# Score products over 128 contraction rows: padded low parts of the keys and padded rotary tiles

## The chip, the core and the metric

The kernel runs on one core of a Trainium2 chip. Its engines are TensorE (matrix products; PE in the profile, its weight loads PEld), VectorE (DVE), ScalarE (ACT), GpSimd (POOL) and SyncE (SP), which issues most of the transfers. The metric is the device time of one execution in microseconds; the median of the runs counts.

## The reference

A sequence of 512 tokens with 1024 channels passes through two small transformer blocks of two layers each. Each layer is a mixer and a gated feed-forward net with a convolution of width three. The mixers are a state-space layer (S5), the Fox attention, a chunk attention and a latent attention (MLA). All three attentions have 16 heads of 64 channels. Their scores, in short:

```python
# Fox: causal, with a decay per head and position
s = einsum('bhqd,bshd->bhqs', q, k) + F[q] - F[k];  p = softmax(where(causal, s, -inf))
# chunk attention: a bias by distance, keys of the own and the earlier chunks
s = einsum('bhqd,bkhd->bhqk', q, k) * 64**-0.5 + bias;  p = softmax(where(valid, s, NEG_INF))
# MLA: 64 channels of each head and 32 rotary channels, whose key is one for all heads
s = (einsum('bqhd,bkhd->bhqk', qn, kn) + einsum('bqhd,bkd->bhqk', qr, kr)) * 96**-0.5
```

In each the probabilities then multiply the values, and the result is projected back to 1024 channels.

## The kernel before

Activations lie with channels on the 128 partitions and the 512 tokens along the columns. Every product is taken with operands split into a rounded high part and a low part that holds the rest. The large projections add three products (high by high, high by low, low by high; `mm3`, lines 373 to 375).

For the scores, a head has only 64 channels, and the three terms are packed. `proj_q` makes one tile per head: the high part of q on the head's own half of the partitions (64 rows) and the low part on the other half. `proj_k` makes a tile `y` per head with the high part of k on both halves, so that one product over 128 rows (line 561) gives high by high and low by high. The remaining term, high q by low k, is a product over 64 rows (line 565) that reads the head's half of q's tile and of `z`, a tile that holds the low parts of both heads of a pair. In MLA a product over 96 rows (line 564) stands between them: rotary query `r` (32 rows high, 32 low, 32 high again) by rotary key `kr` (64 rows high, 32 low). `Head.scores` does this for four query blocks; block `qb` sees 128 * (qb + 1) keys, so the products have 128, 256, 384 and 512 columns. All terms of a block add up in one bank of the accumulation memory. VectorE then adds bias and mask and takes the maximum (lines 570, 573, 576), ScalarE takes the exponential (586), VectorE normalises (592), and `values` transposes the probabilities (605, ScalarE copies them at 608) and multiplies them with the values (615, products with 64 output columns).

`Mixer` sets the order: 16 heads in 8 pairs, a pair's values after the first scores of the next pair, and after each head 1.5 (Fox, chunk) or 1.75 (MLA) units of projection for later pairs. A unit is one `proj_q`, one `proj_k`, half a `proj_v`, or in MLA a `uqr`, which makes the rotary queries of four heads. The order within each engine is fixed when the program is built; an engine works through its own queue in that order and waits at an instruction until its operands and its buffer are there.

The tiles of q, k, v and the rotary queries come from the pool `gp` with 28 buffers of 128 x 512; in Fox and chunk attention the results of the heads lie there too, in MLA the latent inputs. ScalarE writes the high part (line 520), GpSimd copies it to the other half (521), VectorE subtracts for the low part (522). In `uqr` the same three are lines 1526, 1527 and 1528.

Of the kernel before, what the change touches and what calls it, by code (L numbers as in the profile page):

```python
# [9 lines left out]
F32 = mybir.dt.float32  # L10
F32R = mybir.dt.float32r
# [75 lines left out]
def tile_two_blocks(ctx, tc, ap, out):  # L87
# [15 lines left out]
    # ---------------------------------------------------------------- constants  # L103
# [20 lines left out]
    # ---------------------------------------------------------------- adaLN columns  # L124
# [15 lines left out]
    def ada(name, first, cb, m, bias, key, n=24):  # L140
        """Queue one layer's columns: shift and scale, then the gate."""
        items = ada_items(name, first, n, cb, m)
        for part, a, b in (("", 0, min(16, n)), ("gate", 16, n)):
            if a < b:
                def done(a=a, b=b, part=part):
                    dve.tensor_add(m[:, a:b], m[:, a:b], bias[:, a:b])
                    finished.add(key + part)
                background.extend(items[a:b] + [done])
# [12 lines left out]
    # ---------------------------------------------------------------- rms norm  # L161
    class Norm:
        """Running sum of squares over channel tiles, then 1/rms spread over all partitions."""
# [55 lines left out]
    class TwoNorms(Norm):  # L219
        """A norm with gains g, and 1/rms of its result times that of the norm itself."""  # L220
# [56 lines left out]
    def modulate(h, rb, A, B, alloc=None):  # L277
        """(h * rstd) * A + B per channel tile, as hi and lo parts."""
        X = []
        for k in range(len(h)):  # L280
            a, b = A[:, k:k + 1], B[:, k:k + 1]
            t = tmp.tile([P, S], F32, name="t0")
            hi, lo = (alloc or pair)()
            dve.scalar_tensor_tensor(t, h[k], a, rb, op0=OP.mult, op1=OP.mult)  # L284
            act.activation(hi, t, AF.Identity, bias=b)
            if k % 2:
                dve.scalar_tensor_tensor(lo, t, b, hi.bitcast(F32), op0=OP.add, op1=OP.subtract)
            else:
                v = tmp.tile([P, S], F32, name="t1")
                act.activation(v, t, AF.Identity, bias=b)  # L290
                pool.tensor_tensor(lo, v, hi.bitcast(F32), OP.subtract)  # L291
            X.append((hi, lo))
        return X
# [4 lines left out]
    class Ahead:  # L298
        """Products with A h taken while 1/rms is on its way: W^T (r A h + B) = r W^T (A h) + W^T B."""
# [15 lines left out]
        def products(self, jobs, norm=None):  # L315
            """jobs: (pool, name, weights) each."""
# [30 lines left out]
    # ---------------------------------------------------------------- weights  # L347
# [29 lines left out]
    def gemm(ps, src, kts, X, cols=P, eng=dve, seq=None, shift=None, then={}, loaded=None):  # L377
        """ps[cols, S] (+)= W^T X for the channel tiles kts; src is the DRAM tile [P, len * cols]."""
# [31 lines left out]
    # ---------------------------------------------------------------- load x, c  # L410
    h = [hp.tile([P, S], F32, name=f"h{k}") for k in range(KD)]

    def affine(m, shift, scale, g, name):
        """A = g * (1 + scale)"""
        A = late[0].tile([P, KD], F32, name="A_" + name)
        dve.scalar_tensor_tensor(A, m[:, scale:scale + KD], 1.0, g, op0=OP.add, op1=OP.mult)
        return A, m[:, shift:shift + KD]

    def project_out(src, X, gate, norm=None, ready=None, early=0, perm=False):
        """h += gate * (W^T X); ready() gives what the next products need, asked for before channel tile early."""  # L420
# [22 lines left out]
    # ---------------------------------------------------------------- feed-forward  # L443
    def ffn(gp, ahead, norm, wup, wdn, cw, cb, both, gate, last, aside=None):
        """cw(tap, channel tile) and cb(channel tile) give columns; both: the second half is convolved too."""
# [41 lines left out]
    # ---------------------------------------------------------------- attention  # L487
# [7 lines left out]
    def start_attention(ahead, norm, *srcs):  # L495
        """The first projections before 1/rms, then the modulated input."""
        ps = ahead.products([(pl, name, w) for w, (pl, name) in zip(srcs, ((ps_mm, "mm"), (ps_s, "s")))],
                            norm)
        X = modulate(h, ahead.rb, ahead.A, ahead.B)
        return X, [lambda i=i, p=p: ahead.value(p, i) for i, p in enumerate(ps)]  # L500

    def proj_q(ps, scale):
        """Per head of a pair: hi rows at the head's own half of the partitions, lo rows at the other."""
# [9 lines left out]
    def proj_k(ps):  # L513
        """Per head hi rows on both halves; lo rows of both heads in one tile."""
        z = gp.tile([P, S], F32R, name="g")
        out = []
        for hh in range(2):
            a, b = HALF[hh], HALF[1 - hh]
            y = gp.tile([P, S], F32R, name="g")
            act.activation(y[a], ps[a], AF.Copy)  # L520
            pool.tensor_copy(y[b], y[a].bitcast(F32))
            dve.tensor_sub(z[a], ps[a], y[a].bitcast(F32))
            out.append(y)
        return out, z

    def proj_v(src, kts, X, half, wts):
        """Token-major values of two pairs of heads, for the two token tiles of a half."""
# [18 lines left out]
    class Head:  # L546
        """One head: scores and softmax, then transposed probabilities times values."""

        def scores(self, hh, x, y, z, bias, bias_d, scale, extra=None, fq=None):
            a = HALF[hh]  # L550
# [6 lines left out]
            for qb in range(4):  # L557
# [7 lines left out]
                pe.matmul(s, x[a, qs], z[a, :n], start=False, stop=True)  # L565
# [28 lines left out]
    def values(heads, v, cols, dst):  # L594
        """Transposed probabilities times values for a pair of heads, each on its half of the partitions."""
# [24 lines left out]
    class Mixer:  # L620
        """Pairs of heads: a pair's values after the next pair's first scores, projections of later pairs in between."""
# [32 lines left out]
    # ---------------------------------------------------------------- polynomial helpers  # L654
    def stt(eng, work, out, a, c, b, op0, op1):
        """(a op0 c) op1 b"""
# [7 lines left out]
    def sincos(eng, pl, x, shape, tag, work=None, s=None, v=None):  # L664
        """(sin x, 1 - cos x) with x fp32."""
# [39 lines left out]
    # ================================================================ block 1, layer 0: S5  # L705
# [5 lines left out]
    class Later:  # L711
        """Stands for an engine: keeps its instructions for a chosen place among others."""
# [7 lines left out]
    def merge(*lists):  # L720
        """Issue lists of instructions side by side, each spread evenly."""
# [4 lines left out]
    with tc.block(schedule_with_timeline_sim=TIMELINE):  # L726
# [35 lines left out]
        # the input, and shift and scale of its modulation: a quarter of the row on each quarter of the partitions  # L762
# [20 lines left out]
        # parameters: Lambda^a, the factor of B, the rotations of the chunks  # L783
# [48 lines left out]
        # 1/rms  # L832
# [6 lines left out]
        # e^{i 8 theta n}, n < 64: groups 8 q .. and 32 + 8 q .. on the two halves of the partitions  # L839
# [85 lines left out]
        def rotations(q, dve):  # L925
# [4 lines left out]
            for i in range(6):  # L930
                m = 1 << i
                for a in range(2):
                    # real part: c re - s im; imaginary part: c im + s re
# [11 lines left out]
        class Tables:  # L945
            """Tables of groups 8 i .. 8 i + 7."""
# [35 lines left out]
            def for_c(self, eng):  # L982
                """C L^a, a = 0 .. 8"""
# [3 lines left out]
            def for_b(self, eng):  # L987
                """B L^(7 - j)"""
# [17 lines left out]
            def on_pe(self):  # L1006
# [6 lines left out]
                # kernels of the lags 0 .. 7, then shifted copies of them  # L1013
# [20 lines left out]
        def inputs(tab, U):  # L1034
            """What every chunk adds to the states, and the same with real and imaginary parts swapped."""
# [8 lines left out]
        def states(tab, sab):  # L1044
            """The states at the chunks' ends in the turning frame."""
# [15 lines left out]
        def back(tab, wz):  # L1061
            """... and rotated back."""
# [139 lines left out]
    def more_weights(n):  # L1202
        """Room for more tiles of weights while no heads are at work."""
# [45 lines left out]
    # ================================================================ block 1, layer 0: FFN  # L1249
# [12 lines left out]
    # ================================================================ block 1, layer 1: Fox  # L1262
# [20 lines left out]
    # log sigmoid(x) = min(x, 0) - 2 atanh(e / (2 + e)), e = exp(-|x|)  # L1283
# [37 lines left out]
    def qkv_units(wq, wk, wv, X, scale, first):  # L1321
        """Projection units in the order in which the heads need them: src(i) per pair, src(j) per two pairs for v."""
# [18 lines left out]
    def fox_head(t, cur):  # L1341
# [7 lines left out]
        cur.scores(hh, Q[i][hh], K[i][0][hh], K[i][1], b, bd, 1.0, fq=Fq[:, :, t])  # L1349
# [14 lines left out]
    # ================================================================ block 1, layer 1: FFN  # L1364
# [15 lines left out]
    # ================================================================ block 2, layer 0: chunk attention  # L1380
# [17 lines left out]
    def chunk_head(t, cur):  # L1398
# [5 lines left out]
        cur.scores(hh, Q[i][hh], K[i][0][hh], K[i][1], bias_t.pop(t), None, 1.0)  # L1404
# [20 lines left out]
    # ================================================================ block 2, layer 0: FFN  # L1425
# [23 lines left out]
    # ================================================================ block 2, layer 1: MLA  # L1449
# [3 lines left out]
    def rope(t, dst):  # L1453
        """Rotated by the angles of the positions."""
# [33 lines left out]
    kr = rp.tile([96, S], F32R, name="kr")  # L1488
# [29 lines left out]
    def uqr(j):  # L1518
# [4 lines left out]
        for a in range(4):  # L1523
            r = gp.tile([P, S], F32R, name="g")
            src = ps[32 * a:32 * a + 32]
# [35 lines left out]
    def mla_head(t, cur):  # L1561
        i, hh = t // 2, t % 2
        cur.scores(hh, Q[i][hh], K[i][0][hh], K[i][1], mask0, None, SC, extra=(QR.pop(t)[0:96], kr))
        return V[i // 2]
# [11 lines left out]
    # ================================================================ block 2, layer 1: FFN, final norm  # L1576
    g = col("final_g_2", 0, KD)

    def to_end(src, X, gate):
        """The last two channel tiles by halves of the tokens, so that a half's norm runs beside products."""  # L1580
# [128 lines left out]
```

## Time and profile before

| | |
|---|---|
| median of 3 runs | 2748.35 us (2745.33 to 2751.65) |
| span of the profiled execution, first to last instruction | 2740.6 us |
| busy: TensorE matmuls | 2601.1 us, 95% |
| busy: VectorE, ScalarE, GpSimd | 1791.4 us (65%), 1144.3 us (42%), 359.8 us (13%) |
| mean granted clock of TensorE | 0.968 of full |

The profile shows one execution. Its own time was not recorded beside its span; the span is some 8 us under the median of the runs, and that difference is what lies around the first and the last instruction. Matmuls overlap and their ends are modelled, so the busy time of TensorE says how long something was under way, not how fast it went; the distance between two starts tells the latter.

### The profile page before, as it was taken

To read this page: it belongs to the slowest core of one execution; us is meant where nothing else is said; L and a number is where in the kernel's file an instruction comes from. 1 tells how busy PE (TensorE), PEld (TensorE's weight loads), DVE (VectorE), ACT (ScalarE), POOL (GpSimd) and SP (SyncE) were. 2 spreads that over 40 slices of the span, in tenths; PEclk is the share of its full clock that TensorE was granted. 3 is DMA by queue.
4 is the path that set the end of the run, shared out by engine and by line. 5 is a ranking of instruction groups with operands and counts; after the bars stand their busy time and mean duration, and the time that the engine had idled before them with its cause. 6 is when DMAs were issued, how large, how long until landed. Compare 5 with 4: busy or idle time off the path is not lost.

```text
span 2740.6 us, 32676 instructions
## 1 busy us (share of the span) xinstructions
PE 2601.1 (95%) x11970; PEld 2026.6 (74%) x11970; DVE 1791.4 (65%) x3199; ACT 1144.3 (42%) x1904; POOL 359.8 (13%) x331
## 2 busy tenths in 40 slices
PE   3787989999999999999999999999999899999998
PEld 1576768888867767888887777788888566788887
DVE  9897885455576658646566556985766665763554
ACT  2443353233354554323344554532334566542342
POOL 7562100000021100000011010650000110000000
PEclk7878989999999999999999999999999999999999
DMA  5445654443332334455433323445542111323322
GB/s 202 116 119 133 230 183 131 146 142 123 99 108 96 97 107 160 154 168 183 140 105 103 112 92 116 148 150 175 169 140 91 31 35 54 100 86 94 106 78 76
DMA packets 131120, 335.66 MB, mean 122 GB/s; under 512 B 37008, under 2 KB 41872, under 8 KB 130960
## 3 DMA queue, kind: packets, MB, share of 16 engines
q1 hardware_dynamic: 129232, 331.74, 38.4%
q8 instruction: 94, 1.54, 0.2%
q10 hardware_dynamic: 1728, 1.84, 0.2%
q14 instruction: 66, 0.54, 0.1%
HBM read 320.68 MB, written 6.29 MB: 119 GB/s over the span
## 4 chain that ended last, share of the span: by engine, by line
PE 80%; DVE 9%; issue 4%; DMA 2%; POOL 2%; ACT 2%; SPq 0%; POOLq 0%; ACTq 0%; DVEq 0%
PE mm L373 17%; PE mm L374 17%; PE mm L375 17%; PE s L373 6%; PE s L374 6%; PE s L375 6%; PE aux L615 3%; PE pt L605 2%; PE s L565 2%; PE s L561 2%; DMA ada<-in_ada_w_dram 1%; DVE t L284 1%; DVE ada L131 1%; DVE wlo L267 1%; DVE sqa L936 1%
## 5 line engine op out<-in xcount | busy, mean ns | idle before, releaser
L267 DVE TENSOR_TENSOR wlo<-wraw,whi 128x1024 fp32r<-128x1024 f32 (+4 forms) x424 | 464.7, 1096 | 425.8 <-ACT whi L266 420.3
L266 ACT ACTIVATE whi<-wraw 128x1024 fp32r<-128x1024 f32 (+4 forms) x431 | 408.1, 948 | 769.5 <-PE mm L374 579.9
L373 PE MATMUL mm<-hnh,whi 128*128 128x512 f32 x1152 | 468.2, 407 | 36.2 <-ACT hnh L901 27.2
L374 PE MATMUL mm<-hnl,whi 128*128 128x512 f32 x1152 | 463.8, 403 | 7.2 <-POOL hnl L291 3.9
L375 PE MATMUL mm<-hnh,wlo 128*128 128x512 f32 x1152 | 459.5, 399 | 0.1
L373 PE MATMUL mm<-g,whi 128*128 128x512 f32 (+1 forms) x922 | 361.3, 392 | 5.5 <-ACT g L266 3.1
L375 PE MATMUL mm<-g,wlo 128*128 128x512 f32 (+1 forms) x922 | 359.0, 390 | 0.0
L374 PE MATMUL mm<-g,whi 128*128 128x512 f32 (+1 forms) x922 | 358.8, 390 | 0.1
L373 PE MATMUL s<-hnh,whi 128*128 128x512 f32 x720 | 288.4, 401 | 0.0
L373 PEld LDWEIGHTS mm<-hnh,whi 128*128 128x128 f32 x1152 | 219.2, 190 | 91.4 <-ACT hnh L901 27.6
L374 PE MATMUL s<-hnl,whi 128*128 128x512 f32 x720 | 285.4, 396 | 0.0
L375 PE MATMUL s<-hnh,wlo 128*128 128x512 f32 x720 | 284.1, 395 | 0.0
L374 PEld LDWEIGHTS mm<-hnl,whi 128*128 128x128 f32 x1152 | 218.9, 190 | 65.5 <-POOL hnl L291 9.1
L375 PEld LDWEIGHTS mm<-hnh,wlo 128*128 128x128 f32 x1152 | 218.6, 190 | 53.3 <-issue 3.6
L131 DVE SCALAR_TENSOR_TENSOR ada<-ada,cb 128x1024 f32<-128x1024 f32 x192 | 239.3, 1247 | 12.1 <-DMA ada<-in_ada_w_dram 11.7
L373 PEld LDWEIGHTS mm<-g,whi 128*128 128x128 f32 x922 | 173.7, 188 | 46.0 <-issue 4.4
L375 PEld LDWEIGHTS mm<-g,wlo 128*128 128x128 f32 x922 | 173.9, 189 | 39.6 <-issue 2.8
L374 PEld LDWEIGHTS mm<-g,whi 128*128 128x128 f32 x922 | 174.0, 189 | 38.3 <-issue 1.3
L375 PEld LDWEIGHTS s<-hnh,wlo 128*128 128x128 f32 x720 | 135.2, 188 | 32.7 <-issue 0.7
L373 PEld LDWEIGHTS s<-hnh,whi 128*128 128x128 f32 x720 | 135.4, 188 | 30.4
L374 PEld LDWEIGHTS s<-hnl,whi 128*128 128x128 f32 x720 | 135.5, 188 | 29.8 <-issue 0.5
L586 ACT ACTIVATE p<-p,nb 128x128 f32<-128x128 f32 x192 | 105.4, 551 | 68.6 <-DVE nb L581 42.5
(425 smaller groups left out, 3805.3 us busy)
## 6 DMA issues: line engine op xcount, KB each, us to landing
ada<-in_mod_w_dram SPq DMA_DIRECT2D x96, 512.0 KB, 4.1
wraw<-in_ffn_w_up_dram SPq DMA_DIRECT2D x88, 512.0 KB, 3.5
wraw<-in_f_win_dram SPq DMA_DIRECT2D x88, 512.0 KB, 3.5
ada<-in_ada_w_dram SPq DMA_DIRECT2D x80, 512.0 KB, 4.3
wraw<-in_ffn_w_down_dram SPq DMA_DIRECT2D x32, 384.0 KB, 3.1
wraw<-in_f_wout_dram SPq DMA_DIRECT2D x32, 384.0 KB, 3.1
wraw<-in_ffn_w_down_dram SPq DMA_DIRECT2D x32, 320.0 KB, 2.9
wraw<-in_f_wout_dram SPq DMA_DIRECT2D x32, 320.0 KB, 2.9
```

The source lines that it names most:

```text
L131: dve.scalar_tensor_tensor(raw, raw, 1.0, cb, op0=OP.mult, op1=OP.mult, accum_out=dst[:, i:i + 1])
L266: act.activation(hi, v, AF.Copy)
L267: return eng.tensor_tensor(lo, v, hi.bitcast(F32), OP.subtract)
L284: dve.scalar_tensor_tensor(t, h[k], a, rb, op0=OP.mult, op1=OP.mult)
L373: pe.matmul(ps, wh, xh, start=start, stop=False)
L374: pe.matmul(ps, wh, xl, start=False, stop=False)
L375: return pe.matmul(ps, wl, xh, start=False, stop=stop).ins
L561: pe.matmul(s, x[:, qs], y[:, :n], start=True, stop=False)
L565: pe.matmul(s, x[a, qs], z[a, :n], start=False, stop=True)
L586: act.activation(p[:, sl], p[:, sl], AF.Exp, bias=nb[:, qb:qb + 1], scale=scale, accum_out=l[:, qb:qb + 1])
L605: pe.transpose(pt[:, n:n + P], cur.p[:, c:c + P], ident)
L615: pe.matmul(o[HALF[hh], kb * P:], v[kb // 2][:, kb % 2, c], parts[hh][:, n:n + w], start=kb == 0, stop=kb == 2)
```

## The change

The low-part product is taken over all 128 rows. For this each head gets its own tile `z`: the low part of k on the head's half, zeros on the other half, written by GpSimd. The other half of q's tile, which holds the low part of q, meets the zeros. In MLA the rotary tiles get 128 rows instead of 96, the last 32 of them zero. The other lines of the diff take out comments.

```diff
     def proj_k(ps):
-        z = gp.tile([P, S], F32R, name="g")
         out = []
         for hh in range(2):
             a, b = HALF[hh], HALF[1 - hh]
             y = gp.tile([P, S], F32R, name="g")
+            z = gp.tile([P, S], F32R, name="g")
+            pool.memset(z[b].bitcast(F32), 0.0)
             act.activation(y[a], ps[a], AF.Copy)
             pool.tensor_copy(y[b], y[a].bitcast(F32))
             dve.tensor_sub(z[a], ps[a], y[a].bitcast(F32))
-            out.append(y)
-        return out, z
+            out.append((y, z))
+        return out
...
-        def scores(self, hh, x, y, z, bias, bias_d, scale, extra=None, fq=None):
-            a = HALF[hh]
+        def scores(self, x, y, z, bias, bias_d, scale, extra=None, fq=None):
...
-                pe.matmul(s, x[a, qs], z[a, :n], start=False, stop=True)
+                pe.matmul(s, x[:, qs], z[:, :n], start=False, stop=True)
...
-        cur.scores(hh, Q[i][hh], K[i][0][hh], K[i][1], b, bd, 1.0, fq=Fq[:, :, t])
+        cur.scores(Q[i][hh], *K[i][hh], b, bd, 1.0, fq=Fq[:, :, t])
...
-    kr = rp.tile([96, S], F32R, name="kr")
+    kr = rp.tile([P, S], F32R, name="kr")
+    pool.memset(kr[96:].bitcast(F32), 0.0)
...
         for a in range(4):
             r = gp.tile([P, S], F32R, name="g")
+            pool.memset(r[96:].bitcast(F32), 0.0)
             src = ps[32 * a:32 * a + 32]
...
-        cur.scores(hh, Q[i][hh], K[i][0][hh], K[i][1], mask0, None, SC, extra=(QR.pop(t)[0:96], kr))
+        cur.scores(Q[i][hh], *K[i][hh], mask0, None, SC, extra=(QR.pop(t), kr))
```

## Rows read from the trace of the kernel before

**Rows 1.** The page's busy time, share of the span and instructions of each engine.
```profile
span 2740.6 us, 32676 instructions
...
PE 2601.1 (95%) x11970; PEld 2026.6 (74%) x11970; DVE 1791.4 (65%) x3199; ACT 1144.3 (42%) x1904; POOL 359.8 (13%) x331
```

**Rows 2.** The page's chain that ended last, shares by engine.
```profile
PE 80%; DVE 9%; issue 4%; DMA 2%; POOL 2%; ACT 2%; SPq 0%; POOLq 0%; ACTq 0%; DVEq 0%
```

**Rows 3.** Windows: stretch, length; busy us of PE, PEld, DVE, ACT, POOL; PE clock, DMA, GB/s.
```profile
755.00:1010.00 255.00, 245.10 (x1248) 175.13 (x1249) 163.74 (x473) 128.82 (x284) 39.13 (x35) 1.00 0.28 93
1465.00:1690.00 225.00, 223.69 (x1147) 164.49 (x1146) 129.84 (x307) 113.96 (x247) 18.86 (x28) 1.00 0.31 101
2130.00:2330.00 200.00, 188.99 (x821) 120.40 (x821) 130.09 (x344) 120.20 (x280) 18.81 (x30) 0.96 0.13 40
```

**Rows 4.** Chain by line in Fox, chunk and MLA stretches, in this order.
```profile
by line: issue 21.0%; PE mm L375 10.6%; PE mm L373 10.5%; PE mm L374 9.8%; PE aux L615 8.7%; PE pt L605 7.0%; PE s L565 5.0%; POOL t L1348 4.9%; PE s L561 4.1%; DVE p L592 3.0%; DVE wlo L267 1.9%; DVE ada L131 1.8%; ACT whi L266 1.7%; ACT p
by line: PE mm L375 21.1%; PE mm L373 20.7%; PE mm L374 20.4%; PE aux L615 12.4%; PE pt L605 8.5%; PE s L565 8.4%; PE s L561 6.7%; ACT t L608 0.8%; POOL g L521 0.5%; issue 0.4%; ACT g L520 0.3%; ACTq L608 0.0%; POOLq L521 0.0%
by line: PE aux L615 15.4%; PE mm L373 13.6%; PE mm L374 12.2%; PE mm L375 11.5%; PE s L565 10.5%; PE pt L605 9.1%; PE s L561 8.1%; PE s L564 5.6%; ACT t L608 2.2%; PE pt L1456 2.2%; DVE g L1528 1.4%; issue 1.3%; DVE g L1478 1.0%; DVE p L57
```

**Rows 5.** Timeline of matmuls in Fox: start, length, line, operation, rows*columns, operand, count.
```profile
895.16 0.71 PE L605 MATMUL pt<-cc,p 128*128 128x128 f32 x5
895.62 0.31 PE L561 MATMUL s<-g 128*128 128x128 f32 x1
895.86 0.32 PE L565 MATMUL s<-g 64*128 64x128 f32 x1
896.11 0.39 PE L561 MATMUL s<-g 128*128 128x256 f32 x1
...
896.74 0.49 PE L561 MATMUL s<-g 128*128 128x512 f32 x1
...
897.59 0.50 PE L373 MATMUL mm<-hnh,whi 128*128 128x512 f32 x1
897.93 0.39 PE L374 MATMUL mm<-hnl,whi 128*128 128x512 f32 x1
898.16 0.39 PE L375 MATMUL mm<-hnh,wlo 128*128 128x512 f32 x1
```

**Rows 6.** Weight loads of the same stretch.
```profile
897.59 0.19 PEld L373 LDWEIGHTS mm<-hnh,whi 128*128 128x128 f32 x1 [0.24 <-issue]
897.70 0.19 PEld L374 LDWEIGHTS mm<-hnl,whi 128*128 128x128 f32 x1
```

**Rows 7.** Timeline of matmuls: 128 rows, 256 columns.
```profile
812.46 0.28 PE L374 MATMUL mm<-wlo,hnh 128*128 128x256 f32 x1
812.57 0.28 PE L375 MATMUL mm<-whi,hnl 128*128 128x256 f32 x1
```

**Rows 8.** Timeline of one MLA head's score products: the first, and what follows.
```profile
2207.46 0.22 PE L561 MATMUL s<-g 128*128 128x128 f32 x1
...
2210.72 0.70 PE L1456 MATMUL pt<-t,cc 128*128 128x512 f32 x1
```

**Rows 9.** Window of the chunk stretch, low-part products alone (PE, PEld).
```profile
1465.00:1690.00 225.00, 22.57 (x58) 10.23 (x58) 1.00 0.31 101
```

**Rows 10.** Waits (us, times, longest): one of Fox, one of chunk, two of MLA.
```profile
PEld s L561 <- DVE mx L573: 7.3, 12, 1.0
PEld s L561 <- POOL g L521: 1.1, 1, 1.1
POOL g L1527 <- ACT g L1526: 82.7, 15, 19.0
POOL g L1527 <- PE s L565: 0.9, 1, 0.9
```

**Rows 11.** GpSimd's fills by form: line, shape, times, busy us, mean ns.
```profile
L1308 POOL MEMSET nF<- 128x512 f32 x1 | 0.5, 526 | 348.8 <-PE mm L375 348.8
L1304 POOL MEMSET t<- 16x512 f32 x1 | 0.5, 517 | 0.1
```

More of the change, by code (lines that the diff above doesn't have):

```diff
@@ L1403, in chunk_head @@
             load_bias(t + 1)
-        cur.scores(hh, Q[i][hh], K[i][0][hh], K[i][1], bias_t.pop(t), None, 1.0)
+        cur.scores(Q[i][hh], *K[i][hh], bias_t.pop(t), None, 1.0)
         return V[i // 2]
```

## The prediction, as it was put on record

> **What bounds the kernel now.** The first view is the page's list of busy engines: the profiled execution spans 2740.6 us, and TensorE's matmuls fill 95% of it, with VectorE at 65% and ScalarE at 42% [rows 1]. A busy matmul row says little, because matmuls overlap, so the second view is the chain of waits that ended last: 80% of it is TensorE [rows 2]. The third view asks the same of the places that the change touches. Score products run in three stretches only: Fox attention (755 to 1010 us), chunk attention (1465 to 1690; its first head starts some us earlier) and latent attention, MLA (2130 to 2330). In these the matmuls are busy 245 of 255, 224 of 225 and 189 of 200 us, VectorE 58 to 65% and ScalarE 50 to 60%; GpSimd is nearly idle [rows 3]. The chain within each stretch [rows 4] is TensorE for 98% of chunk attention (its seven matmul lines added up) and for 88% of MLA (nine lines). In Fox it is 56%, with 21% "issue", time in which the chain found nothing to wait for. I read that part as TensorE's too, whose matmuls are 96% busy there, so its share is between 56% and 77%. A microsecond taken from TensorE is thus worth nearly its whole in the chunk stretch, and less in Fox.
>
> **What the products cost now.** The fourth view is the timeline of matmuls, read by the distance from one start to the next, since the durations overlap. Products over 128 rows that follow one another start 0.23 us apart at 512 columns (897.93 to 898.16 [rows 5]) and 0.11 at 256 columns [rows 7], for which I use 0.12; five transposes of 128 columns take 0.46 us up to the start of the next line [rows 5], 0.09 each, and I use 0.11 as the cautious figure. At 384 columns I use 0.17, midway between 256 and 512. In such a run the weight load of the next product begins with the start of the one before it and is hidden: L374's load starts at 897.70 [rows 6], 0.23 us before its matmul.
>
> Around a score product over 64 rows it is otherwise. In Fox the L561 (128 rows) and L565 (64 rows) products alternate [rows 5]. At 128 columns the two intervals are 0.24 and 0.25; from one L561 to the next a pair takes 0.49 at 128 columns, 0.63 at 256, and from 896.74 to the L373 that follows 0.85 at 512. The weight load of that L373 starts only at 897.59, together with its own matmul [rows 6]. So a change of row count costs about 0.2 us on the way in and again on the way out (the least at 128 columns): against two 128-row steps 0.27 us a pair at 128 columns, 0.39 at 256 and 0.39 at 512; at 384 I take 0.37. The four query blocks of a head make 1.42 us. The first 128-row product after the return pays again, 0.34 for 0.23 (897.59 to 897.93), because the load of the next was not hidden either.
>
> **The change part by part.** (1) The low-part product L565 goes from 64 to 128 rows. Its columns, its place in the accumulation group and the width of its weights stay, so it should cost what L561 costs among 128-row work. Fox and chunk have 16 heads each: 32 x 1.42 = 45 us. To this come 0.11 us wherever a projection or transpose follows, as after one of the three low-part products of [rows 5]: by that some 43 of 128 places, 5 us. So 50 us for both.
>
> (2) In MLA three products form a group, of 128, 96 and 64 rows. One head's twelve run from 2207.46 to 2210.72 [rows 8], 3.26 us; at 128-row steps (0.11 + 0.12 + 0.17 + 0.23 = 0.63 for the four blocks, three times) they would take 1.89. That is 1.37 too many, 22 us for 16 heads. All three row counts become 128, so all of it goes; how it divides between the 64-row and the 96-row product the rows don't settle.
>
> The steps thus give 72 us. The chain gives a second estimate. In chunk attention L565 and L561 hold 15.1% of 225 us, 34.0 us [rows 4], for the 58 low-part products that fall in the stretch [rows 9]; as many pairs at 128-row steps would be 18.2 us (2 x 16 x 0.63 x 58/64). That leaves 15.8, or 17.4 for all 64. MLA's three lines hold 24.2% of 200, 48.4 us, against 3 x 16 x 0.63 = 30.2: 18.2 us. With Fox like chunk that is 53 us, without the returns, which the chain books to the line that follows: a third of 192 at 0.2, or 13 us. So 66. The steps assume that each low-part product stands as in the rows shown; the chain takes them as they stand, so I take its 66 us of TensorE time, 22 a stretch, with 53 (no returns) and 73 (the steps) as bounds.
>
> The Trainium skill would set the 128-row steps lower. TensorE: Matmul & The Clock Gate, "Back-to-back issue gap", gives columns/2.4 GHz plus some 2.5 ns: as an estimate 0.06, 0.11, 0.16 and 0.22 us, 0.55 a head where the rows give 0.63. By it the sum would be larger by 0.08 for each of (32 x 2 + 16 x 3) sets of four products, 9 us, 75 by the chain's way. The rows have a weight load with every product and decide.
>
> (3) Of this the share that reaches the end is TensorE's share of each stretch's chain: 22 x 0.77 + 22 x 0.98 + 22 x 0.88 = 58 us; with Fox at 0.56 it would be 53. The rest I expect back as new short waits of TensorE, above all L561 for the score bank that VectorE frees (7.3 us in Fox now [rows 10]).
>
> (4) Added zeros: GpSimd writes 48 half tiles (two per K pair, 24 pairs), 16 strips of 32 rows for the rotary queries and one for the rotary key, all 512 columns: 65 instructions. The fills in the trace take 0.53 us for 128 x 512 and 0.52 for 16 x 512 [rows 11], whatever the rows; so 0.53 each, 34 us in all, 8.5 in Fox, 8.5 in chunk, 17 in MLA. GpSimd was busy 39, 19 and 19 us there [rows 3], so it stays under a fifth. Each zero is written ahead of the copies that the scores need (L521, L1527). What hides it is GpSimd's idle time: in MLA it waits for ScalarE 83 us in all before L1527 [rows 10]. Without that cover each would move its copy by 0.53, at most 34 us; below nothing it cannot go, as it removes no work. The row nearest to exposure is TensorE's wait for GpSimd's copy, 1.1 us, once in chunk [rows 10]. I take 2 us.
>
> (5) A K pair now holds four tiles of the 28-buffer pool instead of three. Counting live tiles along the written order, Fox and chunk stay at 21 at most; MLA goes from 26 to 27. The trace has one wait of GpSimd for a score product, 0.9 us [rows 10], which is how a missing buffer would look. I take nothing, with rival three as its bound. (6) ScalarE and VectorE do the same instructions, and no DMA is added or moved.
>
> 58 - 2 = 56. The profiled execution spans 2740.6 and the median of the runs is 2748.35, so some 8 us lie around the span and are not touched: 2748.35 - 56 = 2692.
>
> **The rivals.** First, the gain is half lost: VectorE and ScalarE form a softmax chain per head (scores, maximum, exponential, normalisation, transposes), and a TensorE that comes 1.4 us a head earlier meets results that don't. For it speak the 21% "issue" and the 4.9% of GpSimd's L1348 in Fox's chain [rows 4]; against it that in chunk 98% of the chain is matmuls and that VectorE has a third of its time free. Time: 66/2 - 2 = 31 off, 2717.
>
> Second, the padding does nothing: the slow steps come from something else that these products share, their accumulation group or their columns. For it speaks that L561 and L565 come as a pair; against it that L373 to L375 accumulate into one bank too and step by 0.23. The zeros remain: 2748 + 2 = 2750.
>
> Third, the other side: in MLA one spare buffer is left where there were two. Each zero that opens a K tile then waits at the head of GpSimd's queue until an older head's score product has read its tile; the copies L521 and L1527 behind it come late, and the scores after them. A head takes 200/16 = 12.5 us; a wait of one head in each of 8 pairs is 100 us, less the 56: 2792. It decides from 56/8 = 7 us a pair on; waits of 0.9 would not show.
>
> The Trainium skill also has a rule against GpSimd work beside VectorE (SBUF — State Buffer, "Practical consequences"): an instruction of VectorE in a two-port mode and one of GpSimd exclude each other for their whole length. By it 65 zeros could hold up VectorE by at most their 34 us, spread over 680, and with 0.15 of such time reaching the end the sum would be 5 us smaller. No row here shows a fill doing so.
>
> **How the numbers follow.** The forecast, 2680 to 2706 by the spread of 53 to 73 us and the shares of the chain, gets 0.66. Half lost has 0.18, no effect 0.06, the buffer wait 0.07. More than the forecast has 0.03: the granted clock in MLA is 0.96 of full [rows 3], which is 16 of 200 us at the lower level of 1.2 GHz, and a denser TensorE could win back up to 8 us. A measurement of this kernel tells about 0.2%, 5.5 us, from no change. Faster is 0.66 + 0.18 + 0.03 = 0.87, same 0.06, slower 0.07. The range from 2675 (the full 73 us) to 2728 takes in the first rival with as much spread as the forecast; it leaves out some 0.15.
>
> **What would show it.** L561 and L565 of one query block should start 0.11, 0.12, 0.17 and 0.23 us apart, with the weight load of the second beginning at the start of the first, and MLA's three alike. The three stretches should shorten by 17, 21 and 19 us and nothing else by more than a microsecond or two. Waits of TensorE for L573, L576 and L608 may grow by some 10 us. The prediction is wrong if the intervals stay at 0.3 to 0.4, if they fall while a stretch keeps its length, or if GpSimd's zeros wait for L565 and TensorE for L521 or L1527 behind them.

## The result

| | before | after |
|---|---|---|
| median, runs | 2748.66 us, 4 (2745.33 to 2751.65) | 2697.28 us, 4 (2696.06 to 2699.05) |
| ratio, 95% interval | | 0.9823, 0.9807 to 0.984 |
| span of the profiled execution | 2740.6 us | 2695.9 us |
| its own time | not recorded | 2697.69 us |
| mean granted clock of TensorE | 0.968 | 0.971 |

The change makes the kernel 51 us faster; 2692 was forecast. Later comparisons on three chips, with 55 runs of before (median 2741.33 us) and four more of after, gave a smaller gain; the last section shows how little of that the clock explains.

The page of the kernel after, busy time by engine (it answers to [rows 1]):

```profile
span 2695.9 us, 32723 instructions
...
PE 2545.3 (94%) x11970; PEld 2017.1 (75%) x11970; DVE 1794.2 (67%) x3199; ACT 1143.3 (42%) x1904; POOL 393.1 (15%) x396
```

TensorE has as many products as before and is busy 56 us less, GpSimd has 65 instructions and 33 us more, and the other two do what they did. The same engines in windows laid around the moved stretches, Fox, chunk and MLA (columns as in [rows 3]):

```profile
745.00:1000.00 255.00, 238.82 (x1298) 179.51 (x1297) 174.07 (x485) 135.67 (x294) 50.59 (x53) 1.00 0.30 99
1430.00:1665.00 235.00, 229.10 (x1244) 178.81 (x1245) 147.51 (x339) 123.47 (x264) 30.64 (x48) 0.99 0.32 106
2105.00:2285.00 180.00, 166.52 (x814) 115.02 (x813) 130.18 (x339) 119.03 (x280) 32.80 (x58) 0.97 0.15 44
```

In Fox and MLA VectorE and ScalarE are a larger share of the stretch than in [rows 3] (MLA 72% and 66%, against 65% and 60%), TensorE a smaller one (MLA 92.5% against 94.5%, Fox 94% against 96%).

Where the time came from is read with one mark per layer: the sums of squares for each norm are products of line 198, and from one such to the next the trace gives the length of each mixer and each feed-forward net.

| us | before | after | difference |
|---|---|---|---|
| S5, feed-forward | 330.8, 381.7 | 330.4, 380.0 | -0.4, -1.7 |
| Fox, feed-forward | 302.8, 376.6 | 292.4, 375.6 | -10.4, -1.0 |
| chunk, feed-forward | 289.9, 375.3 | 277.6, 375.3 | -12.3, 0.0 |
| MLA, feed-forward | 273.6, 388.7 | 254.6, 388.7 | -19.0, 0.0 |

The three attentions carry 41.7 of the 44.7 us between the spans. Forecast were 17, 21 and 19: MLA got shorter by what was forecast, Fox and chunk by some six tenths of it. Now the steps. The matmuls of one MLA head, which answer to [rows 8]:

```profile
2135.18 0.23 PE L561 MATMUL s<-g 128*128 128x128 f32 x1
2135.24 0.27 PE L564 MATMUL s<-kr,g 128*128 128x128 f32 x1
2135.36 0.28 PE L565 MATMUL s<-g 128*128 128x128 f32 x1
2135.47 0.33 PE L561 MATMUL s<-g 128*128 128x256 f32 x1
2135.64 0.27 PE L564 MATMUL s<-kr,g 128*128 128x256 f32 x1
2135.75 0.28 PE L565 MATMUL s<-g 128*128 128x256 f32 x1
2135.87 0.40 PE L561 MATMUL s<-g 128*128 128x512 f32 x1
2136.11 0.40 PE L564 MATMUL s<-kr,g 128*128 128x512 f32 x1
2136.34 0.40 PE L565 MATMUL s<-g 128*128 128x512 f32 x1
2136.57 0.33 PE L561 MATMUL s<-g 128*128 128x384 f32 x1
2136.74 0.34 PE L564 MATMUL s<-kr,g 128*128 128x384 f32 x1
2136.92 0.35 PE L565 MATMUL s<-g 128*128 128x384 f32 x1
2137.11 0.22 PE L561 MATMUL s<-g 128*128 128x128 f32 x1
```

From 2135.18 to 2137.11 the twelve products take 1.93 us, where they took 3.26 and 1.89 was forecast. But this is a head at its best. The following one is from chunk attention, matmuls and then weight loads (in brackets the idle time in front of an instruction, and what ended it):

```profile
1515.43 0.22 PE L561 MATMUL s<-g 128*128 128x128 f32 x1
1515.49 0.28 PE L565 MATMUL s<-g 128*128 128x128 f32 x1
1515.60 0.33 PE L561 MATMUL s<-g 128*128 128x256 f32 x1
1515.77 0.28 PE L565 MATMUL s<-g 128*128 128x256 f32 x1
1515.89 0.81 PE L561 MATMUL s<-g 128*128 128x512 f32 x2
1516.54 0.57 PE L565 MATMUL s<-g 128*128 128x384 f32 x2
```

```profile
1515.43 0.19 PEld L565 LDWEIGHTS s<-g 128*128 128x128 f32 x1
...
1516.25 0.19 PEld L561 LDWEIGHTS s<-g 128*128 128x128 f32 x1 [0.29 <-DVE mx L576]
```

The first two pairs take 0.46 us together, as forecast, and the weight load of the first L565 starts with the L561 in front of it, at 1515.43, so it is hidden. The second L565 is less punctual: it starts 0.17 us behind its L561, where 0.12 was forecast. Then the fourth L561 of the head waits 0.29 us until VectorE has taken the maximum of an earlier block and its bank is free. Waits of this kind were there before; for L576 they have grown from 2.8 to 10.3 us in all.

### The profile page after: what moved, and what is told of

It is laid out like the page before. It is cut to its first block, busy times and chain, and to the rows that moved or that the text cites. A ratio compares the mean times of both kernels' runs of the same rounds, so it can differ in the third digit from the quotient of the medians.

```text
span 2695.9 us, 32723 instructions
## 1 busy us (share of the span) xinstructions
PE 2545.3 (94%) x11970; PEld 2017.1 (75%) x11970; DVE 1794.2 (67%) x3199; ACT 1143.3 (42%) x1904; POOL 393.1 (15%) x396
## 5 line engine op out<-in xcount | busy, mean ns | idle before, releaser
L373 PE MATMUL mm<-hnh,whi 128*128 128x512 f32 x1152 | 467.1, 405 | 41.4 <-ACT hnh L901 30.9
L131 DVE SCALAR_TENSOR_TENSOR ada<-ada,cb 128x1024 f32<-128x1024 f32 x192 | 239.3, 1247 | 10.6 <-DMA ada<-in_ada_w_dram 10.4
L473 ACT ACTIVATE t<-t 128x512 f32<-128x512 f32 x88 | 55.5, 631 | 185.8 <-DVE t L450 176.4
```

What stands on the lines that cost most here:

```text
L131: dve.scalar_tensor_tensor(raw, raw, 1.0, cb, op0=OP.mult, op1=OP.mult, accum_out=dst[:, i:i + 1])
L373: pe.matmul(ps, wh, xh, start=start, stop=False)
L473: act.activation(sa, ya, AF.Silu)
```

## The experiments

My theory: TensorE pays for each change between 64 and 128 contraction rows, the change removes these steps, and part of the gain comes back as waits for VectorE and ScalarE, which are no faster. The rivals: the padded rotary tiles matter too; the count of 64 rows itself, not its change, is what is slow; the zeros cost something; the lost part is VectorE's quantity of work. Every kernel was measured beside runs of before on the same chip.

**Each half alone.** e1 pads only the low parts, e2 only the rotary tiles:

```diff
# e1, from the kernel after
-    kr = rp.tile([P, S], F32R, name="kr")
-    pool.memset(kr[96:].bitcast(F32), 0.0)
+    kr = rp.tile([96, S], F32R, name="kr")
-            pool.memset(r[96:].bitcast(F32), 0.0)
-        cur.scores(Q[i][hh], *K[i][hh], mask0, None, SC, extra=(QR.pop(t), kr))
+        cur.scores(Q[i][hh], *K[i][hh], mask0, None, SC, extra=(QR.pop(t)[0:96], kr))
# e2, from the kernel before
-    kr = rp.tile([96, S], F32R, name="kr")
+    kr = rp.tile([P, S], F32R, name="kr")
+    pool.memset(kr[96:].bitcast(F32), 0.0)
...
+            pool.memset(r[96:].bitcast(F32), 0.0)
...
-        cur.scores(hh, Q[i][hh], K[i][0][hh], K[i][1], mask0, None, SC, extra=(QR.pop(t)[0:96], kr))
+        cur.scores(hh, Q[i][hh], K[i][0][hh], K[i][1], mask0, None, SC, extra=(QR.pop(t), kr))
```

> The padded low part alone; the rotary tiles keep their 96 rows, and the 17 zeros for them are gone. If only the step between 64 rows and more is slow, and 96 rows count like 128, everything stays: 2690 to 2698 us, a ratio to the kernel before of 0.981 to 0.983, and the step from L561 to L564 is 0.11, 0.12, 0.17 and 0.23 us at 128 to 512 columns. If each row count is a state of its own that has to be entered and left, the rotary products keep some 0.1 us on the way in and out, 64 x 0.2 = 13 us: about 2710, ratio 0.986.

> The padded rotary tiles alone; the low parts keep 64 rows. If 96 rows already count like 128: no gain, the zeros cost 0 to 2 us, 2748 to 2751 us, ratio 1.000 to 1.001. If each row count is a state of its own: a third of MLA's gain, 4 to 7 us off, ratio 0.9975 to 0.9985, with the step from L561 to L564 falling from 0.34 to 0.23 us at 512 columns.

e1 took 2701.74 us, ratio 0.985 (0.9831 to 0.9868); e2 2738.65, ratio 0.9982 (0.9971 to 0.9993). The low parts carry the gain. By its number e2 lies where a gain of the rotary padding was expected, but its trace doesn't show the step that was to fall: from L561 to L564 it is 0.34 us at 512 columns, as before, and MLA's score products take 62.6 us in all (from start to next start), 60.9 before. Matmuls of e1 in MLA, a projection and a score block of 384 columns:

```profile
2200.73 0.40 PE L375 MATMUL mm<-g,wlo 128*128 128x512 f32 x1
2200.96 0.34 PE L561 MATMUL s<-g 128*128 128x384 f32 x1
2201.14 0.34 PE L564 MATMUL s<-kr,g 96*128 96x384 f32 x1
2201.32 0.34 PE L565 MATMUL s<-g 128*128 128x384 f32 x1
2201.49 0.39 PE L373 MATMUL mm<-g,whi 128*128 128x512 f32 x1
```

A product over 96 rows between two over 128 steps by 0.18 us in and 0.18 out, as those over 128 rows do (0.17 and 0.18 in the MLA head above, 2136.57 to 2136.92). So a change from 128 to 96 rows costs nothing, and in MLA all of the slow steps were the 64-row product's. The Trainium skill lists row tilings of 128, 64 and 32 rows and says that changing the mode drains the engine (TensorEngine Tiling (Array Packing), "Tiling Modes" and "Key Properties"). By that rule 96 rows would be no mode of their own, and the trace agrees.

**The zeros alone.** e3 keeps the tiles and the zeros of the kernel after but multiplies over 64 and 96 rows, as before:

```diff
-                    pe.matmul(s, r[:, qs], kr[:, :n], start=False, stop=False)
-                pe.matmul(s, x[:, qs], z[:, :n], start=False, stop=True)
+                    pe.matmul(s, r[0:96, qs], kr[0:96, :n], start=False, stop=False)
+                pe.matmul(s, x[HALF[hh], qs], z[HALF[hh], :n], start=False, stop=True)
```

> All tiles and zeros of the change, but the products take 64 and 96 rows as before, so only the costs of the change are in it. If the zeros and the fourth tile are hidden: 2748 to 2752 us, ratio 1.000 to 1.0015. If part of the gain that did not come (56 forecast, 51 measured, 66 expected on TensorE alone) went into the zeros or into waits for buffers: 5 to 15 us more than before, ratio 1.002 to 1.0055, the most of it in MLA, where the changed kernel has GpSimd waiting 15 us for L561 in front of the zeros.

It took 2745.35 us, ratio 1.0008 (0.9996 to 1.0019): 2 us more, between 1 less and 5 more, which can't be told from nothing. The order of the instructions on every engine is that of the kernel after, so what differs between e3 and after is the row count alone. The waits of the weight loads (in all, times, longest), first in e3:

```profile
PEld s L565 <- issue: 27.1, 105, 0.8
PEld aux L615 <- ACT t L608: 17.3, 54, 1.2
...
PEld s L561 <- DVE mx L573: 7.7, 12, 1.3
...
PEld s L561 <- DVE mx L576: 4.6, 13, 0.6
```

and in the kernel after:

```profile
PEld aux L615 <- ACT t L608: 29.0, 81, 1.5
...
PEld s L561 <- DVE mx L573: 12.6, 14, 1.8
...
PEld s L561 <- DVE mx L576: 10.3, 23, 1.2
...
PEld s L565 <- DVE g L523: 2.6, 3, 1.0
...
PEld s L565 <- issue: 1.4, 4, 0.4
```

Two things are read here. The 27.1 us of idle time in which the load of a 64-row product started late for no visible reason have shrunk to 1.4: these are slow steps. And with nothing else changed the waits for the maxima go from 12.3 to 22.9 us, those of the values for ScalarE's copies from 17.3 to 29.0: 22 us of waits have come in. This is idle time of the weight loads, which run ahead of their products, so the products need not be late by all of it.

GpSimd's zeros in the kernel after (busy, mean ns of one, idle in front and for what):

```profile
L520 POOL MEMSET g<- 64x512 f32 x48 | 25.4, 529 | 20.5 <-PE s L561 15.0 <-PE mm L374 3.8
L1526 POOL MEMSET g<- 32x512 f32 x16 | 7.9, 522 | 8.3 <-PE aux L615 4.6 <-PE s L561 3.4
```

Their price of 0.53 was right. Four times a zero waits for L561 of an old head (15.0 us): the third rival's mechanism. In e3 the same row has 18.5 us, at no cost that can be told, so these waits are covered.

**Half the changes of rows.** e6 keeps the products over 64 rows and orders them two and two; `hi` holds lines 561 and 564:

```diff
+            def hi(qb):
...
-                pe.matmul(s, x[a, qs], z[a, :n], start=False, stop=True)
+            def lo(qb):
+                n = (qb + 1) * P
+                pe.matmul(banks[qb], x[a, qb * P:n], z[a, :n], start=False, stop=True)
+            for qb in range(4):
+                n = (qb + 1) * P
+                if qb % 2 == 0:
+                    hi(qb), hi(qb + 1), lo(qb), lo(qb + 1)
+                s = banks[qb]
```

> The kernel before with its 64-row products, but written in another order: high parts (and rotary products) of two query blocks, then the low parts of both. If the step between row counts is what costs, the number of steps halves: of some 45 us in the score products 15 to 22 go, 2726 to 2735 us, ratio 0.992 to 0.995, unless the scores wait more for their banks. If a 64-row product is slow by itself, wherever it stands: no change, ratio 0.999 to 1.002.

2726.64 us, ratio 0.994 (0.9924 to 0.9956): 17 us off with the same products over the same rows, half as many changes of row count. That supports the change of rows as the cause and speaks against 64 rows being slow by itself; it doesn't exclude that the new order helps in another way, too. The starts in e6's trace answer more directly. A 64-row product that follows another, of 128 columns, starts 0.16 us behind it (43 places), where in the kernel before a 128-row product starts 0.25 us behind one of 64 rows; four such pairs of 128-row low parts in the kernel after take 0.16, 0.16, 0.06 and 0.06. At 384 columns something is left: two of 64 rows lie 0.28 us apart (7 places), two of 128 rows 0.17 (5 places in the kernel after). So the change is the larger part, and a smaller one may belong to 64 rows as such.

**Fewer zeros.** e4 takes four fixed tiles per attention for the low parts, whose zero halves are written once at its start; e5 is e4 with rotary tiles of 96 rows.

```diff
-            z = gp.tile([P, S], F32R, name="g")
-            pool.memset(z[b].bitcast(F32), 0.0)
+            z = zt[turn_z[0] % 2][hh]
...
+        turn_z[0] += 1
...
-    gp = ctx.enter_context(tc.tile_pool(name="gp", bufs=28))
+    gp = ctx.enter_context(tc.tile_pool(name="gp", bufs=26))
```

> The changed kernel with four fixed tiles for the low parts in each attention, whose zero halves are written once (12 zeros in place of 48), and a pool of 26 buffers in place of 28. If zeros and the waits in front of them (15 us of GpSimd for L561 in MLA) are covered by GpSimd's idle time: as the changed kernel, ratio to the kernel before 0.981 to 0.984. If they hold part of the gain back: 5 to 10 us faster, ratio 0.978 to 0.981.

> The same with rotary tiles of 96 rows and without their 17 zeros. If 96 rows step like 128 (as the timelines of the single parts show) and the 4 us between the low part alone and the whole change are the spread of order and of chips: the same as with fixed tiles alone, within 2 us. If the rotary padding gives something of its own: 4 to 7 us slower than with fixed tiles alone, ratio 0.983 to 0.987.

e4 took 2696.80 us, ratio 0.9841 (0.9826 to 0.9857); e5 2701.25, ratio 0.986 (0.9844 to 0.9876). The two intervals overlap; e4's overlaps that of the kernel after in its first comparison, too, and e5's that of its second (e12, below): 36 zeros fewer are worth at most a few us. By its number e5, 4.5 us above e4, lies where a gain of the rotary padding was expected; e9 below tests that in one order.

**VectorE's quantity of work.** e7 is the kernel before and e8 the kernel after, both without the normalisation (lines 588 to 592): the probabilities are left unscaled. It takes 240 instructions from VectorE.

```diff
-            ri = sml.tile([P, 4], F32, name="ri")
-            dve.reciprocal(ri, l)
-            for qb in range(4):
-                sl = slice(POFF[qb], POFF[qb] + (qb + 1) * P)
-                dve.tensor_scalar(p[:, sl], p[:, sl], ri[:, qb:qb + 1], None, op0=OP.mult)
```

> The kernel before without the normalisation of the probabilities (lines 588 to 592 left out, so its results are not scaled): some 1.8 us of VectorE a head less, 84 us in all, and a shorter way from scores to transposes. It is the base for the next run. If TensorE alone sets the three stretches, it gains 0 to 10 us, 2734 to 2748; if VectorE's chain holds TensorE up, 15 to 30 us.

> The changed kernel without the normalisation, against the kernel before without it. If part of TensorE's 66 us came back as waits for VectorE (waits of L561 for the score banks grew from 7.3 to 12.6 us in Fox), the difference between the two is larger than between the kernels themselves: 56 to 64 us in place of 48 to 51. If the 66 were too many from the start, because some of the slow steps were such waits already and some lie next to the 64-column products of the values, it stays at 45 to 52.

e7 took 2741.12 us, ratio 1.0 (0.9989 to 1.0012); e8 2698.23, ratio 0.9848 (0.9835 to 0.9862). VectorE loses 73 us of work in e7 (1718.8 busy against [rows 1]) and the time stays; with 76 us less, the change gains 42.9 and no more than otherwise. In e8 the waits for the maxima are 13.7 and 8.0 us, against 12.6 and 10.3. So the waits aren't for want of VectorE time. By the kernel's code a bank becomes free when bias, mask and maximum of its own block are done, and that chain is as long as before.

**Rotary width again, in one order.** e1 and e5 came out some 4 us slower than after and e4, and in e1 the order of TensorE's products differs from the second pair of MLA on. e9 keeps tiles, zeros and order and reads 96 rows; e12 is the kernel after once more, on the same chip.

```diff
-                    pe.matmul(s, r[:, qs], kr[:, :n], start=False, stop=False)
+                    pe.matmul(s, r[0:96, qs], kr[0:96, :n], start=False, stop=False)
```

> The changed kernel with all its tiles and zeros, and so with the same order of instructions on every engine, but the rotary product reads only 96 rows. If 96 rows are stepped through like 128 (113, 118, 180 and 233 ns from L564 to L565 in the low part alone), the time is that of the changed kernel within 2 us, and the 4 us between low part alone and whole change came from the order in MLA. If 96 rows cost something of their own: 4 to 7 us more than the changed kernel.

> The changed kernel once more, beside the others of this call on one chip: ratio to the kernel before 0.981 to 0.985.

e9: 2700.92 us, ratio 0.9855 (0.9843 to 0.9868). e12: 2704.79 us, ratio 0.9862 (0.9846 to 0.9878). With 128 rotary rows it was, if anything, slower; the padding of the rotary tiles is worth nothing. e12 surprised: the same kernel, 7.5 us above its first median (last section).

**A bank for two blocks.** Blocks 0 and 2 of a head share a bank; in e10 (from after) and e11 (from before) blocks 0 and 1 share it, and block 2 has one of its own.

```diff
-                s = small[:, :P] if qb == 0 else small[:, P:] if qb == 2 else ps_s.tile([P, S], F32, name="s")[:, :n]
+                s = small[:, :P] if qb == 0 else small[:, P:3 * P] if qb == 1 else ps_s.tile([P, S], F32, name="s")[:, :n]
```

> The changed kernel with query blocks 0 and 1 in one score bank (128 and 256 columns) in place of 0 and 2, so that the next head's block 1 needs no bank of its own. If the gain that did not come went into waits of L561 for VectorE's reductions (10.1 us before, 22.9 after, in the three stretches), these waits fall by a third to a half and the time by 4 to 10 us against the changed kernel, ratio 0.978 to 0.981. If those waits are not what holds TensorE: within 2 us of the changed kernel.

> The same pairing of banks in the kernel before. There TensorE waits only 10 us for score banks, so little is to be had: 0 to 3 us faster, ratio 0.999 to 1.000. With the run on the changed kernel it gives the gain of the padding when banks come earlier: 52 to 58 us if the bank waits ate it, 45 to 51 if not.

e10 took 2702.89 us, ratio 0.9865 (0.9852 to 0.9877); e11 2740.96, ratio 1.0 (0.9991 to 1.0009). The waits for the maxima in e10 are 15.6 and 9.5 us, 25.1 in all, not fewer. The edit failed to remove what it was aimed at, and so leaves open whether the time would follow if it did.

## Why the prediction was right, and where not

**The steps (1, 2).** Right in kind, taken too large in size. Summed over all score products, the time from one's start to the next matmul's start was 145.0 us before and 102.0 after. At the forecast's prices for 128 rows it would be 70.6 (0.63 for a set of four, 32 x 2 + 16 x 3 sets), so 74.4 and 31.4 us lie above. Of these, 14.0 us before and 19.4 after lie in front of a matmul whose weight load had waited for another engine. What is left is the slow steps, 60.4 before and 12.0 after: 48 us have gone. To this come the products behind a return to 128 rows: some 57 projections, whose next start came 0.34 us later at 512 columns and 0.22 at 256, and now comes 0.23 and 0.12 later, some 6 us. Together that is 54 us, where 66 was taken and 53 to 73 allowed. Not all of what is left could go: in Fox and chunk an L565 starts 0.17 us behind its L561 at 256 columns and 0.28 at 384 (medians), where the forecast had 0.12 and 0.17; why, no run shows. The product behind L565 comes after 0.11, 0.12, 0.17 and 0.23, as forecast. The formula that the forecast quotes from the Trainium skill (TensorE: Matmul & The Clock Gate, "Back-to-back issue gap") stands there for an isolated product; for products in a row, as here, the 0.64 a set of the MLA head above (1.93 for three) bears out the rows' 0.63 and not the 0.55.

**The share that reaches the end (3).** This is the other term that was mis-sized. The three attentions are 41.7 us shorter. By the clock records of the two traces they spent 34 us at the lower clock before and 24 after, which is worth 5; so some 37 us are the change's, and of the 54 some 17 came back as waits, where 8 were taken. The trace has places for them: inside the score products the waits rose by 5 us (14.0 to 19.4), the idle time of weight loads in front of a run of score products by 8 (14.9 to 23.1), and the values' products (L615) take 3 us more. The shares of the chain of before told where TensorE was the last to end, but not by how little: a score bank, or a transposed copy, that was ready a tenth of a us ahead before, can be late now. The forecast named the places, L573, L576 and L608, and gave them some 10 us; the idle time of weight loads there grew by 21. By stretches the score products' sums fell by 15.0, 13.7 and 14.3 us in Fox, chunk and MLA, waits included, and those of the values' products rose by 2.2 and 2.2 and fell by 1.2. So MLA's larger gain isn't in its score products: some 3 us are its clock (17 us at the lower level before, 10 after), the transposes (L605) take 2.5 us less and the projections 1.2, and why they do I can't say. The comparison of e3 with after shows that the faster steps alone bring the waits in; that they cost this much at the end is argued from the sum, not shown, because e10 didn't take them away.

**Zeros (4) and buffers (5).** 2 us were taken, e3 measures 2, within -1 to 5. GpSimd does wait for buffers now, four times for L561, where nothing was expected; it is hidden.

**The baseline.** Some 8 us were said to lie around the span. In every later run it is 1.8 (2697.69 and 2695.9). So the profiled execution of before took some 2742 us and the runs shown were slower ones. 2740.6 + 1.8 less 56 would have been 2686, 11 us under the result: the surplus of the baseline covered half of what the two terms missed. That the forecast of 2692 came within 6 us is partly luck.

**The division in MLA.** The forecast left open how it falls between the 64-row and the 96-row product. The latter has nothing of it (e1, e2, e9).

**The rivals.** That the padding does nothing, and that MLA's buffers turn the sign, are out. "Half lost" had the right mechanism, a softmax chain that TensorE overtakes, and gave 31 us off. At equal clock (below) the gain is 39, nearer to that rival than to the forecast's 56; the direct comparison's 51 is nearer to the forecast. What the runs settle is faster, by 35 to 51 us; that some third of the steps' gain was lost in waits (17 of 54) is the account of one pair of traces.

## What to carry to other kernels

A short product over 64 rows between products over 128 can cost more in its two changes of row count than in its work: look for a weight load that starts with its own matmul instead of with the one before, and pad it to the common count, or group the odd ones, where padding isn't to be had. A product over 96 rows needed no padding here. Before pricing such a gain by its share of the chain, look how early the banks and copies come that the faster engine will ask for next; what is just in time now may be waited for.

## What was not expected of the hardware

Two profiles of one program on one core differ by 9.7 us, about what their granted clock accounts for. The kernel after was profiled at 2695.9 us of span and a mean clock of 0.971, and, as e12, at 2705.6 and 0.967. With two levels, 2.4 and 1.2 GHz, that is 2 x 0.029 x 2695.9 = 156 and 2 x 0.033 x 2705.6 = 179 us at the lower one; at that level work takes nearly twice as long (rows below), so half of the 23 us, 11, is lost, and 9.7 is the difference of the spans. One place at the lower level is the start of MLA in e12, matmuls:

```profile
2131.52 0.30 PE L564 MATMUL s<-kr,g 128*128 128x128 f32 x1 [1.82 <-DVE g L1530]
...
2133.65 0.41 PE L561 MATMUL s<-g 128*128 128x128 f32 x1 [0.39 <-DVE mx L576]
...
2137.03 0.63 PE L373 MATMUL mm<-g,whi 128*128 128x512 f32 x1
2137.45 0.63 PE L374 MATMUL mm<-g,whi 128*128 128x512 f32 x1
...
2140.80 0.40 PE L374 MATMUL mm<-g,whi 128*128 128x512 f32 x1
2141.03 0.39 PE L375 MATMUL mm<-g,wlo 128*128 128x512 f32 x1
```

and the windows of the same stretch (the clock is the third number from the end):

```profile
2130.00:2134.00 4.00, 2.09 (x11) 1.58 (x12) 3.74 (x10) 2.79 (x6) 1.39 (x3) 0.97 0.23 66
2134.00:2138.00 4.00, 3.66 (x12) 2.88 (x12) 3.81 (x13) 2.67 (x5) 2.01 (x4) 0.50 0.00 0
2138.00:2142.00 4.00, 4.00 (x15) 3.34 (x14) 2.01 (x9) 2.12 (x9) 1.51 (x3) 0.68 0.01 2
```

TensorE had waited 1.82 us for the rotary tiles and then 0.39 for a bank; from 2133.65 to 2140.55 its products step nearly twice as far apart (0.42 for 0.23 at 512 columns), at a granted clock of 0.50, which is the level of 1.2 GHz. If the waits brought the clock down, they cost more than their length; but that is read from the order of the two alone, and no run tests it. The kernel after's first profile has such spells at the start of MLA, too: 10 us at the lower level in MLA, against 14 in e12.

Over the 141 runs whose clock is known, of thirteen kernels, a fit with one mean for each kernel and one slope for all gives 1.8 us less for each 0.001 of mean clock, with 2 us left over. At equal clock the kernel after is 38.6 us (37 to 40.2) under before, e1 36.0, e9 38.0, e4 41.4, e8 40.3, e6 14.1, and e3 0.4, all at 1.3 to 2.2 us either way; e2 is 2.8 (1.5 to 4.1) under, a small gain whose place I didn't find. The first comparison's 51 us and e12's 35 are one kernel pair: the intervals, 0.9807 to 0.984 and 0.9846 to 0.9878, don't overlap. The clock explains little of that. The first four runs of after had a mean clock of 0.9698 and e12's four 0.9688, worth 1.8 us, where their means lie 5.8 us apart; and the first four runs of before, whose median is 7 us above that of the 55 later ones, have no clock on record. What else moved, the chip perhaps, stays open. The interval of one comparison doesn't take in what moves between comparisons.
